# Gate stores on ScalarE and a rewritten order of the middle stage in a hybrid recurrence and pooling decoder layer

## The chip, the cores and the metric

One Trainium2 chip, one core. The metric is the time of one execution on the device in microseconds (us). Where a kernel was run several times, the median is given with the lowest and the highest. One further execution was recorded by the hardware profiler, and every duration below is from that record.

The engines go by these names: PE is the matrix engine, DVE the vector engine, ACT the scalar engine (activations and casts), POOL the general one, SP the one whose queue issues most transfers (DMAs) between the chip's memory and the core.

## What is computed

One decoder layer on 1024 tokens with 16 learned ones ahead of them, model width 1024, everything in float32:

```python
u = rmsnorm(h, mix_norm_pre)
q, f_logit, i_in, g_out, v_pool, gate_a, gate_b = split(u @ w_in)
a = hgrn2(q, f_logit, i_in, g_out, ...)      # 4 heads of 128: gated recurrence, chunked; then a norm per head, times sigmoid(g_out)
p = multiscale_pool(v_pool, pool_proj, ...)  # 4 groups of 128: trailing mean of 2, 4, 8, 16 minus identity, then a 128x128 projection
z = sigmoid(gate_a) * (a @ w_branch_hgrn) + sigmoid(gate_b) * (p @ w_branch_pool)
h = h + rmsnorm(z @ w_out, mix_norm_post)
u = rmsnorm(h, ffn_norm_pre)
y = (gelu(causal_dwconv(u @ ffn_w_gate)) * (u @ ffn_w_up)) @ ffn_w_down   # width 2816
h = h + rmsnorm(y, ffn_norm_post)            # the first 16 tokens are dropped
```

## The kernel before, in words

**Number format and tiles.** A float32 product is made of three matmuls on a high and a low part of each operand (L186 to L188, L206, L207, L210). The high part is a cast, mostly on ACT, the low part a subtraction, mostly on DVE (L832 and L833 for activations, L152/L153, L162/L163 for weights). The tokens lie along the free dimension of a tile in three chunks of about 342 to 348, each with a PSUM bank of its own (a bank holds the sums that PE writes; there are eight), and the channels lie in blocks of 128 on the partitions.

**Stages.** First the norm of the input and the projections to i. Then the gate stage, up to 326 us: f, q and the two branch gates, gate_a and gate_b, by a class `Strassen` that makes seven half-size products for eight. For each piece that is done, `put_gate` (L852 to L870) adds the partial results on DVE, applies the sigmoid on ACT (L868) to a branch gate, and has SP store the piece in the chip's memory (L870): q to `qscr`, the branch gates to `sscr`, 32 such stores. They are loaded again much later by `load_gate`. For f, `put_f` makes the decay f, the key k and kb, a product that the first level needs, and stores them. Then comes the middle stage that the change rewrites, 326 to some 650 us; after it w_out, the second norm and the feed-forward part.

**The middle stage.** PE runs in the order in which the program is written; the orders of ACT, DVE, POOL and SP are made by a scheduler that sees when things become due. The PE order is the string `ORDER` (L56 to L60). The loop at L1139 to L1178 takes a word at a time:

- `h<i>` is one more step of head i, a generator (`head_steps`, L653 to L803). It has twelve: the loads of f, q, kb and k by SP (L656 to L659), which are held until the last gate weights (for heads 0 and 1) or the last stage weights are loaded; the first level (`sb`, L719, 32x32 blocks; before it DVE multiplies q by f, L714); six levels with blocks of 2 to 64 (`sl`, L690 and L696), each of them followed by a growth of q, k and f on DVE (L673, L677, L679, L681) and a masked copy of the scores (`near`, L711); transposes (`pt`, L751); the state (`ds`, L761 to L771); the output (`po`, 34 matmuls, L781 to L794); and the norm (`ms`, L798 and L799), Ln and Exp on ACT (L800, L801), and a product on DVE (L802). L832 and L833 split o.
- `PV` is the projection of a pool group, 54 matmuls; `PVp` to `PVs` are its quarters with 18 each. `post_pv` (L809) copies the banks and makes the running sum; `sp` splits the pooled value.
- `G` is the output gate's projection of a head (quarters as above).
- `PP` is the 128x128 projection of a pool group: 9 matmuls, then ACT writes the high part (L841) and DVE the low one (L842), both to `phis`.
- `BB` and `BA` are the two branch projections, a block of 128 outputs each (`a` and `b` are halves); `post_branch` (L879) multiplies by the loaded gates `sa`. `BA` adds both.
- `sa<i>` splits head i's output for `BA`.
- `w<i>` has nothing to do with this stage: it makes ahead of time the high and low parts of weights that the feed-forward stage will need (`keep_first`, `keep_unit`, L906 to L965; DVE does L920 and L923, ACT casts at L922). `pay` (L937) stores them in memory, as `kept0` to `kept10`, through SP's queue.

In the old order the whole of PV0 (108 matmuls) stands ahead of the first head step, the four `PP` have up to two head steps between them and the `w` of the first group stand between the last `PP` and the first `BB`.

Of the kernel before, what the change touches and what calls it, by code (L numbers as in the profile page):

```python
# [11 lines left out]
AF = mybir.ActivationFunctionType  # L12
# [7 lines left out]
KD = D // P  # L20
# [32 lines left out]
ZA = 4  # L53
AHEAD = 3

ORDER = ("h0 h1 PV0 PVp1 PVq1 h0 PVr1 h1 PVs1 h0 PVp2 h1 PVq2 h0 sp0 PVr2 h1 PVs2 h0 PVp3 h1 sp1 PVq3 h0 PVr3 h1 "  # L56
# [4 lines left out]
POOLED = ()  # L61
VLOAD = 8
TRUNC = False
# [6 lines left out]
def trunk_kernel(ctx: ExitStack, tc: tile.TileContext, x, meta_tokens, mix_norm_pre,  # L70
# [3 lines left out]
    nc = tc.nc  # L74
    act, dve, pool_e, pe = nc.scalar, nc.vector, nc.gpsimd, nc.tensor
# [24 lines left out]
    def slot(n, dtype=F32, name="s"):  # L100
        return stage["fm", "p"].tile([P, n], dtype, tag="fm", name=nm(name), padded_shape=[P, LP])
# [114 lines left out]
    class Strassen:  # L216

        ORDER = ("P1", "P2", "P6", "P5", "P3", "P7", "P4")
        MOVING = dict(P1="b11", P2="b21", P3="b22", P4="t4", P5="t1", P6="t2", P7="t3")
        SECOND = ("P3", "P5", "P7")  # L220

        def __init__(self, units, run, early, quarters, base, halo, put, whole):
# [6 lines left out]
            for u in run:  # L229
                self.seq += [(u, p) for p in self.ORDER if u >= early or p not in ("P1", "P2")]  # L230
            self.got, self.at, self.kept, self.begun = [], 0, [], {}
# [385 lines left out]
    qdr = dram.tile([HEADS, P, TQ], F32, name="qscr")  # L617
# [12 lines left out]
    def put_f(m, half, g):  # L630

        n = HN if half else HF
        both = slot(2 * HP, name="fk")
        f, k = both[:, :n], both[:, HP : HP + n]
        act.activation(f, g, AF.Sigmoid)
        act.activation(k, g, AF.Sigmoid, scale=-1.0)
        dve.tensor_scalar(f, f, oml[:, m : m + 1], lb[:, m : m + 1], ALU.mult, ALU.add)
        dve.tensor_scalar(f, f, LOG_FLOOR, None, ALU.max)
        act.activation(k, k, AF.Copy, scale=oml[:, m : m + 1])
        t0 = NM + (HF if half else 0)  # L640
        for t, d in ((f, fdr), (k, kdr)):
            nc.sync.dma_start(d[m][:, t0 : t0 + n], t)
            if not half:
                nc.sync.dma_start(d[m][:, :NM], t[:, :NM])
        f2, k2 = (t[:, n - HN :].rearrange("p (b two) -> p b two", two=2) for t in (f, k))
        kb = g[:, n - HN :]
        b2 = kb.rearrange("p (b two) -> p b two", two=2)
        act.copy(b2[:, :, 0], k2[:, :, 0])
        dve.reciprocal(b2[:, :, 1], f2[:, :, 1])
        dve.tensor_tensor(b2[:, :, 1], b2[:, :, 1], k2[:, :, 1], ALU.mult)  # L650
        nc.sync.dma_start(kbdr[m][:, half * HN : half * HN + HN], kb)
# [197 lines left out]
    sd = dram.tile([2 * KD, P, TQ], F32, name="sscr")  # L849
# [3 lines left out]
    def ghalo(u):  # L853
        return NM if GUNITS[u][0] == "F" else HALO

    def put_gate(u, i, h, a, b, c=None):
        kind, j = GUNITS[u]
        m, n = 2 * j + i, ghalo(u) + HN
        at = slice(n, n + HN) if h else slice(0, n)
        g = slot(at.stop - at.start, name="sg")  # L860
        dve.tensor_tensor(g, a, b, ALU.add)
        if c is not None:
            dve.tensor_tensor(g, g, c, ALU.add)
        if kind == "F":
            put_f(m, h, g)
            return
        if kind != "Q":
            act.activation(g, g, AF.Sigmoid)  # L868
        to = dict(Q=qdr, A=sd, B=sd)[kind]
        nc.sync.dma_start(to[m + (KD if kind == "B" else 0), :, at], g)  # L870

    def load_gate(d, b, m):
        d[m] = slot(TQ, name="sa")
# [33 lines left out]
    BEGUN = [(e, p) for es in ((0, 1), (2, 3, UP0)) for p in ("P1", "P2") for e in es]  # L907
    KEPT = BEGUN + [(u, p) for u in (0, UP0) for p in Strassen.ORDER[2:]]
    kept = [[dram.tile([P, 1024], F32, name=f"kept{t}{h}") for h in "hl"] for t in range(len(KEPT) // 2)]
# [54 lines left out]

    order = ORDER.split()  # L965
    order = [(o_[:-1], int(o_[-1])) for o_ in order]
# [23 lines left out]
    def gate_steps(d):  # L990
# [10 lines left out]
        else:  # L1001
# [18 lines left out]
    ds = [slice(0, NM)] + [slice(NM + i * P, NM + (i + 1) * P) for i in range(4)]  # L1020
    gates = Strassen([(WIN, dict(F=CF, Q=CQ, A=CA, B=CB)[k] + 2 * P * j) for k, j in GUNITS], range(len(GUNITS)),
                     EARLY, gq, NM, ghalo, put_gate, lambda u, i: None)

    vb = [bank("pv") for _ in range(2)]
# [114 lines left out]
    with tc.manual_schedule(engines={E.PE}):  # L1139
        for kind, i in order:  # L1140
# [14 lines left out]
            kind, part = kind.rstrip("abpqrs"), kind[-1]  # L1155
# [548 lines left out]
    with tc.manual_schedule(engines={E.Activation, E.DVE}):  # L1704
        for s_ in range(3):
            banks = [[bank("pd") for _ in range(NT)] for _ in range(2)]
            for k in range(KH):
                at = s_ * KH + k
# [97 lines left out]
```

## Time and profile before

| what | value |
|---|---|
| time, median of 3 runs | 1319.91 us (1318.8 to 1320.88) |
| the profiled execution's own time | 1317.88 us |
| its span in the profile | 1316.2 us |
| busy PE | 1290.6 us (98%) |
| busy DVE | 961.2 us (73%) |
| busy ACT | 522.5 us (40%) |
| busy POOL | 359.9 us (27%) |
| clock granted to PE | 0.995 of full |

How to read it: the profile is of one execution, whose time is 1.68 us more than its span. PE is busy nearly all of the time, so a group of instructions on another engine counts only where PE waits for it. The share of a DMA window says how busy the sixteen transfer engines of the core were: 1.00 means full.

### The profile page before, as it was taken

To read this page: it belongs to the slowest core of one execution; us is meant where nothing else is said; L and a number is where in the kernel's file an instruction comes from. 1 tells how busy PE (TensorE), PEld (TensorE's weight loads), DVE (VectorE), ACT (ScalarE), POOL (GpSimd) and SP (SyncE) were. 2 spreads that over 40 slices of the span, in tenths; PEclk is the share of its full clock that TensorE was granted. 3 is DMA by queue.
4 is the path that set the end of the run, shared out by engine and by line. 5 is a ranking of instruction groups with operands and counts; after the bars stand their busy time and mean duration, and the time that the engine had idled before them with its cause. 6 is when DMAs were issued, how large, how long until landed. Compare 5 with 4: busy or idle time off the path is not lost.

```text
span 1316.2 us, 21988 instructions
## 1 busy us (share of the span) xinstructions
PE 1290.6 (98%) x8650; PEld 1139.7 (87%) x8650; DVE 961.2 (73%) x1293; ACT 522.5 (40%) x904; POOL 359.9 (27%) x307
## 2 busy tenths in 40 slices
PE   8999999999999899999999999999999999999998
PEld 7799899998998788978898888888888888888887
DVE  6768965454685887675588999888988985455758
ACT  5554533333134737226564222222332223444443
POOL 3015333230000000160035555554755652000000
PEclk9999999999999899999999999999999999999999
DMA  8135543334524566876677776667677699666644
GB/s 275 42 106 173 197 156 103 107 105 138 174 71 147 193 225 215 291 235 250 237 256 248 193 211 185 172 196 192 167 180 172 131 267 300 208 224 224 225 174 161
DMA packets 143802, 247.62 MB, mean 188 GB/s; under 512 B 11000, under 2 KB 75164, under 8 KB 143698
## 3 DMA queue, kind: packets, MB, share of 16 engines
q1 hardware_dynamic: 131634, 221.83, 49.6%
q0 software_dynamic: 12064, 24.38, 11.0%
q8 instruction: 68, 1.11, 0.3%
q14 instruction: 36, 0.29, 0.1%
HBM read 174.11 MB, written 95.09 MB: 205 GB/s over the span
## 4 chain that ended last, share of the span: by engine, by line
PE 91%; DVE 3%; DMA 2%; ACT 2%; issue 1%; SPq 0%; DVEq 0%; ACTq 0%
PE P L306 17%; PE P L307 17%; PE P L309 17%; PE pd L186 5%; PE pd L188 5%; PE pd L187 5%; PE pm L186 2%; PE pm L188 2%; PE pm L187 2%; PE ppv L206 1%; PE ppv L210 1%; PE pg L206 1%; PE ppv L207 1%; PE pv L187 1%; PE pv L186 1%
## 5 line engine op out<-in xcount | busy, mean ns | idle before, releaser
L307 PE MATMUL P<-v,whi 128*128 128x512 f32 (+2 forms) x408 | 140.7, 353 | 0.0
L306 PE MATMUL P<-v,whi 128*128 128x512 f32 (+2 forms) x408 | 140.7, 352 | 0.0
L309 PE MATMUL P<-v,wlo 128*128 128x512 f32 (+2 forms) x424 | 135.1, 349 | 0.0
L277 POOL TENSOR_TENSOR swa<-wraw,wraw 128x512 f32<-128x512 f32 x32 | 51.1, 1598 | 186.1 <-DMA wraw<-in_w_in_dram 79.8
L251 ACT CAST whi<-wraw 128x512 fp32r<-128x512 f32 x90 | 53.1, 618 | 102.4 <-PE P L307 75.9
L1516 DVE TENSOR_TENSOR rot<-wraw,rot 128x1024 fp32r<-128x1024 f32 x31 | 38.0, 1224 | 72.3 <-ACT rot L1515 72.3
L306 PEld LDWEIGHTS P<-v,whi 128*128 128x128 f32 x408 | 76.7, 188 | 10.4
L307 PEld LDWEIGHTS P<-v,whi 128*128 128x128 f32 x408 | 76.6, 188 | 10.2
L309 PEld LDWEIGHTS P<-v,wlo 128*128 128x128 f32 x424 | 74.0, 188 | 10.8
L187 PE MATMUL pd<-rot 128*128 128x512 f32 x274 | 82.5, 388 | 0.0
L188 PE MATMUL pd<-rot 128*128 128x512 f32 x274 | 82.5, 388 | 0.0
L186 PE MATMUL pd<-rot 128*128 128x512 f32 x274 | 81.9, 388 | 0.1
L252 DVE TENSOR_TENSOR wlo<-wraw,whi 128x512 fp32r<-128x512 f32 x86 | 76.4, 911 | 2.7 <-ACT whi L251 2.7
L251 ACT CAST whi<-swa 128x512 fp32r<-128x512 f32 x64 | 38.1, 619 | 92.6 <-PE P L307 77.8
L252 DVE TENSOR_TENSOR wlo<-swb,whi 128x512 fp32r<-128x512 f32 x64 | 66.4, 1045 | 10.4 <-ACT whi L251 10.4
L1515 ACT CAST rot<-wraw 128x1024 fp32r<-128x1024 f32 x31 | 32.7, 1054 | 90.8 <-PE pd L188 89.4
L306 PE MATMUL P<-uhi,whi 128*128 128x258 f32 (+2 forms) x240 | 68.5, 303 | 0.0
L307 PE MATMUL P<-ulo,whi 128*128 128x258 f32 (+2 forms) x240 | 68.4, 303 | 0.0
L251 ACT CAST whi<-swb 128x512 fp32r<-128x512 f32 x64 | 38.1, 618 | 71.6 <-PE P L307 67.1
L306 PE MATMUL P<-t4h,whi 128*128 128x258 f32 (+2 forms) x228 | 65.5, 304 | 0.0
L307 PE MATMUL P<-t4l,whi 128*128 128x258 f32 (+2 forms) x228 | 65.4, 304 | 0.0
L306 PE MATMUL P<-t2h,whi 128*128 128x258 f32 (+2 forms) x228 | 65.3, 304 | 0.0
(386 smaller groups left out, 3840.1 us busy)
## 6 DMA issues: line engine op xcount, KB each, us to landing
wraw<-in_w_in_dram SPq DMA_DIRECT2D x36, 512.0 KB, 4.2
yt<-ysum SPq DMA_DIRECT2D x33, 512.0 KB, 5.1
wraw<-in_ffn_w_gate_dram SPq DMA_DIRECT2D x26, 512.0 KB, 6.0
wraw<-in_ffn_w_up_dram SPq DMA_DIRECT2D x22, 512.0 KB, 6.0
wsum<-in_ffn_w_down_dram SPq DMA_DIRECT2D x22, 512.0 KB, 8.5
wraw<-in_w_out_dram SPq DMA_DIRECT2D x18, 512.0 KB, 4.4
ysum<-ys SPq DMA_DIRECT2D x11, 768.0 KB, 5.2
sa<-sscr SPq DMA_DIRECT2D x16, 513.0 KB, 5.3
```

The source lines that it names most:

```text
L186: pe.matmul(ps, ahi, bhi, start=first, stop=False)
L187: pe.matmul(ps, ahi, blo, start=False, stop=False)
L188: pe.matmul(ps, alo, bhi, start=False, stop=last)
L206: pe.matmul(ps[:, :n], whi[:, k, :], xhi, start=(k == 0), stop=False)
L251: act.copy(hi, src)
L252: (pool_e if 4 <= i < 2 * self.early else dve).tensor_tensor(lo, src, rr(hi), ALU.subtract)
L277: pool_e.tensor_tensor(s1, a21, a22, ALU.add)
L306: pe.matmul(d, whi[:, k, :], xh[:, c : c + w], start=(k == 0 and onto is None), stop=False, **go)
L307: pe.matmul(d, whi[:, k, :], xl[:, c : c + w], start=False, stop=False, **go)
L309: pe.matmul(x[:, o : o + w], wlo[:, k, :], xh[:, c : c + w], start=False, stop=(k == 3), **go)
L1515: act.copy(hi, src)
L1516: dve.tensor_tensor(lo, src, rr(hi), ALU.subtract)
```

## The change

Two things. In `put_gate` the store of a branch gate is issued from ACT's own queue, right behind the sigmoid, and no longer from SP's; the store of q stays on SP. And `ORDER` is another string: PV0 is cut in quarters and the first head steps stand after two and three of them; there is one head step between the quarters and between the pool projections; every `BB` is in halves; w0 and w1 stand after `BBb1` and `BBb2`, w4 and w5 later, w2 and w3 next to `BA2` and `BA3`.

```diff
-ORDER = ("h0 h1 PV0 PVp1 PVq1 h0 PVr1 h1 PVs1 h0 PVp2 h1 PVq2 h0 sp0 PVr2 h1 PVs2 h0 PVp3 h1 sp1 PVq3 h0 PVr3 h1 "
...
+ORDER = ("h0 h1 PVp0 PVq0 h0 PVr0 h1 PVs0 h0 PVp1 h1 PVq1 h0 PVr1 h1 PVs1 h0 sp0 PVp2 h1 PVq2 h0 sp1 PVr2 h1 PVs2 "
...
-        if kind != "Q":
-            act.activation(g, g, AF.Sigmoid)
-        to = dict(Q=qdr, A=sd, B=sd)[kind]
-        nc.sync.dma_start(to[m + (KD if kind == "B" else 0), :, at], g)
+        if kind == "Q":
+            nc.sync.dma_start(qdr[m, :, at], g)
+            return
+        act.activation(g, g, AF.Sigmoid)
+        act.dma_start(sd[m + (KD if kind == "B" else 0), :, at], g)
```

The line numbers of the changed kernel are higher by one from here on (L879 is L880 there).

On PE, inside PV0, the rows of the changed kernel (+) against the old one. `ppv` is a bank of the pool projection, `sb_3460` the first level of head 0, `q_3400` and `kb_3399` its loads.

```order
 L210 MATMUL ppv_3414<-uhi_88,wlo_3380 128x346
 L210 MATMUL ppv_3415<-uhi_88,wlo_3380 128x346
+L719 MATMUL sb_3460<-q_3400,kb_3399 32x32 x32
 L206 MATMUL ppv_3413<-uhi_88,whi_3379 128x348
 L207 MATMUL ppv_3413<-ulo_89,whi_3379 128x348
```

The first level of head 0 now stands inside the projection and was behind it before.

On SP, where the loads of head 0 (`f_3397`, `q_3400`, `kb_3399`, `k_3398`) and of head 1 (`f_3405` and on) stand, first before and then in the changed kernel. `sscr` is the memory of the branch gates, `wraw` a weight tile, `vmeta` a few values of the learned tokens.

```order
134 L149 DMA wraw_3488<-in_w_in_dram 128x8x128
135 L870 DMA sscr<-sg_3321 128x512
136 L149 DMA wraw_3666<-in_w_in_dram 128x8x128
137 L870 DMA sscr<-sg_3340 128x512
138 L656 DMA f_3397<-fscr 128x1056
139 L657 DMA q_3400<-qscr 128x1026
140 L658 DMA kb_3399<-kbscr 128x1024
141 L870 DMA sscr<-sg_3369 128x514
142 L659 DMA k_3398<-kscr 128x1056
143 L656 DMA f_3405<-fscr 128x1056
```

```order
105 L149 DMA wraw_3578<-in_w_in_dram 128x8x128
106 L149 DMA wraw_3814<-in_w_in_dram 128x8x128
107 L729 DMA vmeta_3828<-vmscr 16x128
108 L729 DMA vmeta_3895<-vmscr 16x128
109 L656 DMA f_3397<-fscr 128x1056
110 L657 DMA q_3400<-qscr 128x1026
111 L658 DMA kb_3399<-kbscr 128x1024
112 L659 DMA k_3398<-kscr 128x1056
113 L656 DMA f_3405<-fscr 128x1056
```

The gate stores are gone from among the loads, and the loads stand directly behind weight loads and two small loads of head 2 or later.

On DVE, in the stretch of the pool projections, again before and then changed. `phis` is the low part of a pool projection (L842), `k`, `q`, `f` belong to the heads, `o` and `rs` to a head's norm (L802), `al` is the split of a head's output (L833), `wlo` of L163 a branch weight and `wraw` of L923 a weight that is kept.

```order
419 L163 TENSOR_TENSOR wlo_4838<-wraw_4836,whi_4837 128x1024
420 L842 SCALAR_TENSOR_TENSOR phis_4659<-ppp_4806,par,phis_4659 128x342
421 L842 SCALAR_TENSOR_TENSOR phis_4659<-ppp_4807,par,phis_4659 128x342
422 L842 SCALAR_TENSOR_TENSOR phis_4659<-ppp_4808,par,phis_4659 128x342
423 L923 TENSOR_TENSOR wraw_4904<-wraw_4904,whi_4906 128x512 x2
424 L842 SCALAR_TENSOR_TENSOR phis_4659<-ppp_4824,par,phis_4659 128x342
425 L842 SCALAR_TENSOR_TENSOR phis_4659<-ppp_4825,par,phis_4659 128x342
426 L842 SCALAR_TENSOR_TENSOR phis_4659<-ppp_4826,par,phis_4659 128x342
427 L673 TENSOR_TENSOR k_4287<-k_4287,f_4286 128x66x8
```

```order
405 L673 TENSOR_TENSOR k_4566<-k_4566,f_4565 128x528
406 L802 TENSOR_TENSOR o_4532<-o_4532,rs_4533 128x1026
407 L681 TENSOR_TENSOR f_4565<-f_4565 128x528
408 L153 TENSOR_TENSOR wlo_4740<-wraw_4737,whi_4739 128x128
409 L673 TENSOR_TENSOR k_4354<-k_4354,f_4353 128x132x4
410 L679 TENSOR_TENSOR q_4356<-q_4356,f_4353 128x128x4
411 L711 COPY_PREDICATED near_4469<-mask_152,sl_4747 128x32x4
412 L833 TENSOR_TENSOR al_4785<-o_4433,ah_4784 128x1026
413 L681 TENSOR_TENSOR f_4353<-f_4353 128x132
414 L833 TENSOR_TENSOR al_4972<-o_4532,ah_4971 128x1026
415 L153 TENSOR_TENSOR wlo_4803<-wraw_4800,whi_4802 128x128
416 L842 SCALAR_TENSOR_TENSOR phis_4806<-ppp_4788,par,phis_4806 128x342
```

The kept weights' L923 has left the stretch; the head norm's L802 and two splits of L833 stand there ahead of the first subtraction, between steps of heads 2 and 3.

8 rows, old and new, of the table ORDER are left out of this document.

## The prediction

> **What bounds the kernel now.** I began with the page. The span and the timeline of PE, the matrix engine, come first, because the stage that the change rewrites is one in which PE is ordered by hand. I then went through PE's timeline for the whole stage, 326 to 560 us, and took out every matmul that stood behind a wait. The columns are start, duration, engine, line, operation, tile out and in, count, and in brackets the idle time just before and what ended it.
>
> ```profile
> span 1316.2 us, 21988 instructions
> ```
> ```profile
> 326.20 0.40 PE L206 MATMUL ppv<-uhi,whi 128*128 128x348 f32 x1 [0.88 <-DVE sg L861]
> ...
> 343.55 0.76 PE L719 MATMUL sb<-q,kb 128*32 128x32 f32 x64
> ...
> 425.94 0.76 PE L788 MATMUL po<-sc,vh 128*128 128x128 f32 x2 [2.00 <-DVE near L711]
> ...
> 438.14 0.42 PE L798 MATMUL ms<-rh,onesr 128*128 128x342 f32 x1 [2.55 <-DVE phis L842]
> ...
> 440.55 1.06 PE L696 MATMUL sl<-q,k 128*32 128x16 f32 x64 [1.83 <-ACT rs L800]
> ...
> 453.00 0.73 PE L696 MATMUL sl<-q,k 128*32 128x16 f32 x64 [1.51 <-DVE near L711]
> ...
> 453.89 0.42 PE L206 MATMUL pbb<-phis,whi 128*128 128x342 f32 x1 [0.16 <-ACT rs L800]
> ...
> 466.88 1.12 PE L690 MATMUL sl<-q,k 128*64 128x64 f32 x16 [1.65 <-DVE q L679]
> ...
> 492.30 0.39 PE L789 MATMUL po<-q,st 128*128 128x128 f32 x2
> 492.52 0.71 PE L751 MATMUL pt<-ident,k 128*128 128x128 f32 x5
> ...
> 497.29 1.83 PE L768 MATMUL ds<-vh,kt 128*128 128x128 f32 x14 [0.39 <-ACT kt L752]
> ...
> 503.77 0.46 PE L788 MATMUL po<-sc,vh 128*128 128x128 f32 x2 [0.57 <-DVE sa L879]
> ...
> 510.81 0.42 PE L798 MATMUL ms<-rh,onesr 128*128 128x342 f32 x1 [0.42 <-ACT rh L832]
> ...
> 512.41 0.43 PE L799 MATMUL ms<-rl,onesr 128*128 128x342 f32 x1 [1.18 <-DVE rl L833]
> ...
> 552.17 0.43 PE L206 MATMUL pba<-ah,whi 128*128 128x342 f32 x1 [1.19 <-DVE sa L879]
> ```
>
> The brackets sum to 14.33 us. PE has no other wait after its start, so all that this change can win is here, and all that it can lose is a new bracket: the matmuls are the same ones in another order. Three places hold the 14.33. The start of the stage has 0.88. A middle stretch, from the last matmul chunks of the head norms through the pool projections, has 2.00 + 2.55 + 1.83 + 1.51 + 0.16 = 8.05. The tail has 1.65 + 0.39 + 0.57 + 0.42 + 1.18 + 1.19 = 5.40.
>
> A pitch for the path follows from the same rows. Between 326.20 and 343.55 stand the 108 matmuls of PV0, so one takes 17.35 / 108 = 0.161 us. A quarter of 18 is then 2.9, about 3.05 with the change to a narrow tile and back (an estimate), and the 9 of a pool projection 1.45. A small head step of 64 narrow matmuls is taken at 0.7 (0.76 and 0.73 above). The 17 pairs of a head's output go at 492.52 − 492.30 = 0.22 to 0.23 a pair, 4.0 with its beginning.
>
> **The gate stores.** The change moves 32 stores from SP's queue to ScalarE (ACT). Here is one of the last of them with the first load of head 0 behind it and one of head 1's, then the row of the waits that shows what ACT does in that stage (total us, number of waits, longest).
>
> ```profile
> 324.60 0.32 SPq L870 DMA_DIRECT2D sscr<-sg  x1
> 324.97 0.42 SPq L656 DMA_DIRECT2D f<-fscr  x1
> ...
> 329.01 0.54 SPq L658 DMA_DIRECT2D kb<-kbscr  x1
> ```
> ```profile
> ACT whi L251 <- PE P L307: 220.8, 76, 4.4
> ```
>
> Each store stands directly behind its own sigmoid on ACT. It costs ACT 0.32 of issue and an estimated 0.1 for the sigmoid to be seen, so 32 × 0.42 = 13.4 us. What is queued behind it are the weight casts of L251 and L152, which feed PE. ACT idles 220.8 us waiting for PE ahead of those casts, so the 13.4 is covered sixteen times over, and I cost it at 0. If the cover were gone, a single store would delay a cast by 0.42. On SP the removal only frees time: nothing on PE waits on SP in the gate stage. The 0.88 at the start hangs on a DVE addition at L861 that no edit touches, so it stays, rounded to 0.9.
>
> **The first heads, begun 72 matmuls sooner.** 72 × 0.161 = 11.6 us sooner for heads 0 and 1. Their loads were in no hurry before. These are the rows at which they land (the operation that first uses each, with the wait it ended), and then three windows: stretch, its length, busy time of PE, of its weight loads, DVE, ACT and POOL with counts, PE clock, DMA share, GB/s.
>
> ```profile
> 331.51 0.69 DVE L714 TENSOR_TENSOR q<-q,f 128x512 f32<-128x512 f32 x1 [4.04 <-DMA q<-qscr]
> ...
> 335.04 0.71 DVE L673 TENSOR_TENSOR k<-k,f 128x528 f32<-128x528 f32 x1 [2.85 <-DMA k<-kscr]
> ...
> 337.70 0.69 DVE L714 TENSOR_TENSOR q<-q,f 128x512 f32<-128x512 f32 x1 [1.94 <-DMA q<-qscr]
> ...
> 341.97 0.71 DVE L673 TENSOR_TENSOR k<-k,f 128x528 f32<-128x528 f32 x1 [1.02 <-DMA k<-kscr]
> ```
> ```profile
> 322.00:324.00 2.00, 2.00 (x18) 1.92 (x17) 1.37 (x2) 0.06 (x1) 0.00 (x0) 1.00 0.69 179
> 324.00:326.00 2.00, 1.32 (x12) 1.12 (x10) 0.64 (x1) 1.40 (x2) 0.00 (x0) 1.00 1.00 321
> ...
> 334.00:336.00 2.00, 2.00 (x15) 2.00 (x14) 0.71 (x1) 0.00 (x0) 0.10 (x1) 1.00 1.02 414
> ```
>
> PE now reaches head 0's first step (sb, L719) at 326.2 + 36 × 0.161 = 332.0, and head 1's after that step and 18 matmuls, at 335.7. Head 0's q is there at 331.5 and its kb, issued next, lies between 331.5 and k's 335.0. I take 332.3, as kb stands nearer to q: a wait of 0.3. Head 1's kb lies between q's 337.7 and k's 342.0. I take the middle, 339.8. How much sooner it now comes is the doubtful number. SP is free of the six stores ahead of the loads, and their issue can go back from 324.97 to about 323.2, my estimate of when the load gate in front of them opens, since the window of 322 to 324 already has a weight load in it: 1.8 at most. But the DMA share is 1.0 from 324 on, so bytes and not issue set the landing, and only the 0.31 free share of 322 to 324 (0.6 us), with the stores' bytes gone from between the loads, gives something back. I take 1.3, so 338.5, and a wait of 338.5 − 335.7 − 0.3 (PE is already that late) = 2.5. **Sum 2.8**, with bounds of 0.2 (head 1 lands at q's time less 1.8) and 6.3 (it lands at k's 342.0).
>
> In its rules for issuing (DMA: Bandwidth & Descriptors, section "Issuing engines are not separate DMA queues") the Trainium skill says that transfers from whatever engine run on the same 16 DMA engines and interleave, and that a second issuing engine saves the sequencer's time alone. The shares of 1.00 and 1.02 above agree; by that rule alone the move buys nothing here, which is rival A below.
>
> **The middle stretch.** The two DVE weight steps w0 and w1 leave it, and the head steps and the pool projections are interleaved one to one. The prices on DVE and on ACT are these.
>
> ```profile
> 436.38 1.22 DVE L163 TENSOR_TENSOR wlo<-wraw,whi 128x1024 fp32r<-128x1024 f32 x1
> 437.52 1.53 DVE L842 SCALAR_TENSOR_TENSOR phis<-ppp,par,phis 128x342 fp32r<-128x342 f32 x3
> 438.96 1.28 DVE L923 TENSOR_TENSOR wraw<-wraw,whi 128x512 fp32r<-128x512 f32 x2
> ...
> 441.67 0.71 DVE L673 TENSOR_TENSOR k<-k,f 128x528 f32<-128x528 f32 x1
> ...
> 443.77 1.23 DVE L802 TENSOR_TENSOR o<-o,rs 128x1026 f32<-128x1026 f32 x1 [0.58 <-ACT rs L801]
> ...
> 449.99 1.29 DVE L920 TENSOR_TENSOR wlo<-wraw,wraw 128x512 f32<-128x512 f32 x2 [3.59 <-DMA wraw<-in_ffn_w_gate_dram]
> ...
> 452.64 1.26 DVE L833 TENSOR_TENSOR al<-o,ah 128x1026 fp32r<-128x1026 f32 x1
> ```
> ```profile
> 439.95 1.42 ACT L800 ACTIVATE rs<-ms,eps_t 128x342 f32<-128x342 f32 x3
> 441.39 1.28 ACT L801 ACT_TABLE_LOAD   x1
> 442.68 1.06 ACT L801 ACTIVATE rs<-rs 128x1026 f32<-128x1026 f32 x1
> ```
>
> Back to back, an operation takes its duration less some 0.08 (436.38 to 437.52 is 1.14 for a row of 1.22). Two waits come out of this.
>
> First, head 3's first step now follows head 0's norm closely on DVE. From the end of the norm's matmuls run Ln 1.35, table 1.28, Exp 1.0, L802 1.14, then the decay step L681 0.55 and L714 0.6, together 5.95. PE meanwhile has a level step 0.7, a gate quarter 3.05 and the other norm's 6 matmuls 1.0, together 4.7. The wait is 1.25, and I take **1.4** for one crossing between the engines.
>
> Second, from that step to the first branch product BBa0, DVE must do what BBa0's accumulator waits for: the subtractions of PP2 on L842. In its new queue that is 3 × 3 of L842 (3 × 1.45 = 4.35), L802 (1.15), two L833 (2.4), two L163 (2.3), four L673 and three L679 (7 × 0.62 = 4.3), four masks, three decay steps and two small splits of 0.2 to 0.6 (3.4): 17.9, and one crossing of 0.7 with 0.9 of idle while masks wait for PE's levels, 19.5. PE has in the same time the head step 0.7, the last gate quarter 3.05, five small steps at 0.67 and four pool projections at 1.45: 12.9. The waits between sum to **6.6**, whichever instructions show them.
>
> **Sum 8.0**, against 8.05 before. So 3.86 us of weight work (L923 twice, L920 once) is gone from DVE there, but the same stretch of PE is shorter by head steps that are now done earlier, and L802 and both L833 of heads 0 and 1 are now inside it. Lower bound: DVE gets L802 and the two L833 done in its idle time, −3.5, 4.5. Upper bound: ACT reloads its table twice more on the path, 2 × 1.28, 10.6.
>
> On the table load the Trainium skill (ScalarE: Activation LUTs, section "What ACT_TABLE_LOAD costs") has 1283 ns and a drain of 1380 ns more for every switch. The trace agrees with the first alone: the load of 441.39 is followed by Exp at 442.68, 1.29 later, and nothing stands between. With the drain the norm's chain would be 1.4 longer and the forecast 1321.0; the rows decide.
>
> **The tail.** Here the later weight steps and the kept stores matter: name, queue, count, KB each, median us from issue to landing.
>
> ```profile
> kept7h<-whi SPq DMA_DIRECT2D x2, 256.0 KB, 2.0
> kept7l<-wlo SPq DMA_DIRECT2D x2, 256.0 KB, 4.4
> ...
> kept2l<-wraw SPq DMA_DIRECT2D x2, 256.0 KB, 8.1
> ```
>
> The step w4 stands between two steps of head 2 and a branch half, and its L920 waits on DVE for a load, as in the row above (3.59 idle there, no PE wait behind it). I take 0.7 for PE at BBa4, bounds 0 and 3.6. The norm of head 3 then waits for the norm of head 2 and for a weight tile to be stored before DVE may overwrite it. The chain: Ln, table, Exp 3.65, L802 1.15, three sums of L879 1.3 (as L842 × 3), a weight part 0.6, the store 4.4, two more parts 1.3, L794 1.2 and L833 1.1 (both priced as L833): 14.7. PE has two branch halves at 3.0, the output pairs at 4.0 and a third and partial products of another 3.0: 13.0. Wait **1.7**. **Sum 2.4** against 5.40, bounds 0.5 (a store of 2.0 removes the 1.7) and 6.1 (a store of 8.1 adds 3.7).
>
> **The total.** 0.9 + 2.8 + 8.0 + 2.4 = 14.1 us against 14.3: −0.2 to −0.3, so 1317.6 for a run that took 1317.88 when it was profiled. That run lies 1.68 above its span and 2.03 below the median of the three runs, 1319.91. On the scale of the median the forecast is **1319.6 us**, no measurable change (about 0.2%, 2.6 us, is what can be told from none). The three groups' bounds are −2.6/+3.5, −3.5/+2.6 and −1.9/+3.7; they are unlikely to fall together, their squares add to −4.8/+5.7, and the case's own four fifths are some 1316.5 to 1323. With the rivals the range becomes **1315.0 to 1324.0**.
>
> **The rivals.**
> *A, slower: the loads do not come sooner.* The DMA engines are full from 324, so head 1's kb lands as before, at up to 342.0, and the early start runs into it: 6.3 − 2.8 = +3.5, 1323.1. It decides once kb lands after 341. Against it speaks the free share before 324. Chance 0.18.
> *B, slower: the kept store is slow.* At 8.1 instead of 4.4, head 3's norm waits 3.7 longer, 1323.3. It needs landing times over 7; two of the three rows above lie far below. Chance 0.12.
> *C, faster: the weight work was what the stretch waited for.* DVE has 3.86 less to do between 436 and 452, and if all of it comes off the 8.05 there with nothing late next, the time is 1315.7. For it: the waits at 438.14 and 453.00 both name DVE. Against it: ACT's Ln ended 1.83 of it, and the interleave puts L802 and L833 in the place. Chance 0.28.
> That the change does not do what it says is no case: the instructions stand in the order described. Forecast: 0.42. So faster by over 0.2% has 0.28, within 0.2% 0.42, slower 0.30.
>
> **What would show it.** PE's waits at sb of head 1 (2.5, ended by kb's load), at sb of head 3 (1.4), at the pool projections and BBa0 (6.6 together, L842) and at the norm of head 3 (1.7, L833) prove or break each step; so does SP's first L656 at about 323. No wait of PE should name a weight cast delayed by a store. The forecast is wrong if the sum of PE's brackets differs from 14 by over 2.6, and wrong in kind if time appears outside this stage, where PE has none to lose.

## The result and the profile after

The changed kernel takes 1314.48 us (median of 5 runs, 1312.12 to 1315.53) against 1320.25 (5 runs, 1318.80 to 1320.88): a ratio of 0.9955, with a 95% interval of 0.994 to 0.997, 4 to 8 us faster. The forecast was no measurable change, 1319.6, with a range from 1315.0. The profiled execution took 1315.28, so it is one of the slower ones, and the profiled one of before, at 1317.88, was faster than all five of those. The two traces are therefore only 2.6 apart.

PE's timeline of the changed kernel, every matmul that stood behind a wait from 326 us on:

```profile
span 1313.6 us, 21972 instructions
```
```profile
327.30 0.40 PE L206 MATMUL ppv<-uhi,whi 128*128 128x348 f32 x1 [0.88 <-ACT whi L152]
...
335.32 0.75 PE L719 MATMUL sb<-q,kb 128*32 128x32 f32 x64 [2.07 <-DMA kb<-kbscr]
...
342.12 0.75 PE L719 MATMUL sb<-q,kb 128*32 128x32 f32 x64 [1.45 <-DMA kb<-kbscr]
...
431.41 0.90 PE L719 MATMUL sb<-q,kb 128*32 128x32 f32 x64 [2.03 <-ACT rs L800]
...
442.89 0.42 PE L206 MATMUL ppp<-plh,whi 128*128 128x342 f32 x1 [0.99 <-DVE phis L842]
...
444.55 0.39 PE L206 MATMUL ppp<-plh,whi 128*128 128x342 f32 x1 [1.08 <-DVE near L711]
...
447.51 0.65 PE L206 MATMUL ppp<-plh,whi 128*128 128x342 f32 x1 [0.39 <-DVE phis L842]
...
451.15 1.05 PE L696 MATMUL sl<-q,k 128*32 128x16 f32 x64 [0.21 <-DVE near L711]
...
565.99 0.47 PE L186 MATMUL pm<-whi,zc 128*128 128x512 f32 x1 [0.69 <-DVE sa L880]
```

The places of the forecast are all there (heads 0 and 1, head 3, the pool projections), but the tail, from the first branch product at 452 us, has only the 0.69 at its very end.

Brackets alone do not tell the loss. The windows of both kernels show the granted PE clock (third figure from the end of each row). First before, then after:

```profile
425.00:442.00 17.00, 11.67 (x186) 10.94 (x187) 16.31 (x26) 12.95 (x23) 0.95 (x1) 0.82 0.64 210
442.00:452.00 10.00, 9.49 (x110) 8.95 (x109) 5.83 (x11) 4.43 (x7) 0.00 (x0) 0.80 0.66 223
452.00:569.00 117.00, 110.44 (x1028) 106.27 (x1029) 89.72 (x155) 52.35 (x89) 6.14 (x4) 1.00 0.69 235
```
```profile
326.00:340.00 14.00, 11.05 (x119) 10.58 (x118) 6.09 (x8) 1.60 (x2) 2.12 (x6) 0.88 1.00 352
...
425.00:442.00 17.00, 14.87 (x365) 13.72 (x352) 12.62 (x19) 14.66 (x23) 0.18 (x3) 0.90 0.47 155
442.00:452.00 10.00, 7.44 (x150) 5.89 (x150) 10.00 (x21) 7.10 (x13) 0.00 (x0) 0.67 0.87 277
452.00:569.00 117.00, 116.31 (x963) 112.78 (x956) 93.97 (x162) 49.79 (x89) 8.41 (x5) 1.00 0.73 252
```

Behind some of the gaps PE runs at half clock for about 3.4 us or twice that. The shares give what that takes at most (some of the slow time falls into PE's idle time): before 17 × 0.18 + 10 × 0.20 = 5.1 us, after 14 × 0.12 + 17 × 0.10 + 10 × 0.33 = 6.7. The half clock is thus not what the change saved: the changed kernel lost more that way than the old one. With it the stage reads so, from the opening matmul to the first of w_out:

| place | brackets before | half clock before | brackets after | half clock after | forecast after |
|---|---|---|---|---|---|
| heads 0 and 1 begin | 0 | 0 | 3.52 | 1.7 | 2.8 |
| up to the first branch product | 6.38 | 3.1 | 4.70 | 5.0 | 8.0 |
| from there on | 7.07 | 2.0 | 0.69 | 0 | 2.4 |

The forecast's borders differ in one point: it counted the old waits of 1.51 and 0.16, which stand behind the first branch product, in its middle stretch.

The stage itself went from 242.5 us (326.20 to 568.7) to 238.7 (327.30 to 566.0), 3.8 less. What the span holds outside the stage is 1073.7 us before and 1074.9 after, and 1073.6 to 1075.1 in all fourteen traces of this case. Most of the 1.1 us by which the stage opens later has a reason outside the change, one DVE instruction in the gate stage, long before the first gate store (176.46 us on SP before, 177.13 on ACT after). POOL's addition L277 starts beside it. First before, then after:

```profile
112.10 0.56 DVE L637 TENSOR_SCALAR fk<-fk,oml,lb 128x528 f32<-128x528 f32 x1 [0.71 <-ACT fk L635]
...
112.33 1.49 POOL L277 TENSOR_TENSOR swa<-wraw,wraw 128x512 f32<-128x512 f32 x1 [3.59 <-DMA wraw<-in_w_in_dram]
```
```profile
112.02 1.68 DVE L637 TENSOR_SCALAR fk<-fk,oml,lb 128x528 f32<-128x528 f32 x1 [0.71 <-ACT fk L635]
...
112.11 1.30 POOL L277 TENSOR_TENSOR swa<-wraw,wraw 128x512 f32<-128x512 f32 x1 [3.45 <-DMA wraw<-in_w_in_dram]
```

### The profile page after: what moved, and what is told of

Read it like the earlier page. It is cut to its first block, busy times and chain, and to the rows that moved or that the text cites. A ratio compares the mean times of both kernels' runs of the same rounds, so it can differ in the third digit from the quotient of the medians.

```text
span 1313.6 us, 21972 instructions
## 1 busy us (share of the span) xinstructions
PE 1291.5 (98%) x8650; PEld 1140.3 (87%) x8650; DVE 963.7 (73%) x1293; ACT 524.8 (40%) x905; POOL 355.1 (27%) x307
## 4 chain that ended last, share of the span: by engine, by line
PE 92%; DMA 2%; DVE 2%; ACT 2%; issue 1%; SPq 0%; DVEq 0%; ACTq 0%
PE P L306 16%; PE P L307 16%; PE P L309 16%; PE pd L186 5%; PE pd L188 5%; PE pd L187 5%; PE pm L186 2%; PE pm L188 2%; PE pm L187 2%; PE pbb L206 1%; PE pbb L210 1%; PE ppv L206 1%; PE pbb L207 1%; PE pv L187 1%; PE pba L206 1%; PE pba L210 1%
## 5 line engine op out<-in xcount | busy, mean ns | idle before, releaser
L277 POOL TENSOR_TENSOR swa<-wraw,wraw 128x512 f32<-128x512 f32 x32 | 48.2, 1506 | 191.0 <-DMA wraw<-in_w_in_dram 79.4
```

Of the source, the lines that this page charges most:

```text
L277: pool_e.tensor_tensor(s1, a21, a22, ALU.add)
```

## The experiments

Each was profiled and run in five rounds beside the kernel before on the same chip, and the ratios are to that kernel (0.0010 is 1.3 us). Two experiments on different chips are best compared by these ratios. Line numbers can be off by one or by a few where an edit shifts them.

**Stores alone, and the order alone.** The old `ORDER` with the new `put_gate`, and the new `ORDER` with the old `put_gate`.

> The old order, with only the gate stores moved to ScalarE. First theory (the new order alone saves the time; ScalarE has idle time ahead of its casts): within 1 us of the kernel before, PE's waits of the middle stage the same 13 to 14 us and the same three periods at half clock. Rival (the stores out of SP's queue are what helps, since the head loads issue sooner): 2 to 6 us faster than before, with loads of heads 0 and 1 landing over 1 us sooner.

> The new order, with the gate stores left on SP. First theory: as fast as the changed kernel, at most 1.3 us slower, which is what I had put down for the loads of head 1 coming sooner. By the rule that all transfers share the same engines, no difference at all and the same landing of kb. Rival (the stores carry the gain): 3 us or more slower than the changed kernel.

Stores alone: 1319.19, 0.9998 (0.9988 to 1.0007), the first theory. In its trace the loads of heads 0 and 1 are issued 2.2 us sooner than before (324.97 there), and head 1's q lands 0.7 sooner (337.70 there):

```profile
322.75 0.68 SPq L655 DMA_DIRECT2D f<-fscr  x1
...
337.02 0.69 DVE L713 TENSOR_TENSOR q<-q,f 128x512 f32<-128x512 f32 x1 [1.80 <-DMA q<-qscr]
```

Order alone: 1316.23, 0.9974 (0.9963 to 0.9984). Its loads are issued 1.7 us later than the changed kernel's 324.59, and the first levels start at 6.96 and 14.34 from the stage's opening matmul at 327.49 (the changed kernel's at 8.02 and 14.82):

```profile
326.27 0.43 SPq L656 DMA_DIRECT2D f<-fscr  x1
...
334.45 0.75 PE L719 MATMUL sb<-q,kb 128*32 128x32 f32 x64 [1.00 <-DMA kb<-kbscr]
...
341.83 0.75 PE L719 MATMUL sb<-q,kb 128*32 128x32 f32 x64 [3.58 <-DMA kb<-kbscr]
```

Single traces differ more than that. The runs below with the weights put back, with the old tail and with the bunched steps have the words of the changed kernel for heads 0 and 1, and there head 1's first level starts 13.34, 12.94 and 13.00 from the opening, in the changed kernel 14.82. The 14.34 lies among them, so no effect of the issue on kb is shown. The Trainium skill (DMA: Bandwidth & Descriptors, section "Issuing engines are not separate DMA queues") states that issuing from a second engine saves only the time of the issue. The time of the stores alone agrees (0.9998), though head 1's q did land a little sooner there. The order carries the gain; the medians of this run and of the changed kernel are 1.75 apart, between the two theories, but their intervals overlap, so no gain of the stores is shown.

**The first heads later.** The words of PV0 and PV1:

```diff
-h0 h1 PVp0 PVq0 h0 PVr0 h1 PVs0 h0 PVp1 h1 PVq1 h0 PVr1 h1 PVs1 h0 sp0
+h0 h1 PVp0 PVq0 PVr0 PVs0 h0 PVp1 h1 PVq1 h0 PVr1 h1 h0 PVs1 h1 h0 sp0
```

> The changed kernel with the first steps of heads 0 and 1 two quarters (36 matmuls) later, caught up by the end of the second pool projection; everything behind is as in the changed kernel. Theory that the early start is a plain loss (waits of 2.07 and 1.45 for kb, and about 1.7 of half clock after the first of them): 3.5 to 5.2 us faster than the changed kernel. Rival (the catch-up meets DVE and the waits return a few steps later): within 1 us of it.

1310.79, 0.9926 (0.9912 to 0.9940): about 3.8 us faster than the changed kernel, the first theory. Both waits are gone, and the steps that were caught up bring only a gap of 0.50 for which the profile names no cause. Head 3's first level comes 99.07 us after the stage's opening at 326.52, against 104.11. At the end of the stage 2.4 of these 5.0 are left (236.3 us against 238.7): head 3's wait is as it was, half clock runs on to 450.1, some 3.4 us into the branch products, and the last wait is 1.53 against 0.69:

```profile
425.59 0.78 PE L719 MATMUL sb<-q,kb 128*32 128x32 f32 x64 [2.03 <-ACT rs L800]
...
562.79 0.47 PE L186 MATMUL pm<-whi,zc 128*128 128x512 f32 x1 [1.53 <-DVE sa L880]
```

The early start is thus a loss, and the rest of the new order more than pays for it.

**What sets that loss.** Two runs: dummy matmuls in the waits, and head 0's k behind head 1's kb.

```diff
         ps = bank("sb")
+        if h < 2:
+            jb = bank("pj")
+            for _ in range((10, 12)[h]):
+                pe.matmul(jb[:, :P], onesm, ident, start=True, stop=True)
```
```diff
             nc.sync.dma_start(kb[:, M0:], kbdr[h])
-            nc.sync.dma_start(k, kdr[h])
+            late.append((k, kdr[h]))
+            while late and h:
+                nc.sync.dma_start(*late.pop(0))
```

> The changed kernel with matmuls that nobody reads put on PE directly ahead of the first level of head 0 (10) and of head 1 (12), at 0.18 us each (28 of them took 5.16 at the start of the span), in the places where PE stood still for 2.07 and 1.45. Theory that PE's clock is halved for about 3.4 us after such a gap and that this costs 1.7 on top of the bracket: the brackets at both first levels nearly vanish, no period at half clock follows there, and the time falls by about 1.7, less what the filling overshoots the waits by (up to 0.5). Rival (the half clock costs nothing there, or has another cause): the time is as before or up to 0.5 longer, or the period at half clock stays.

> The changed kernel with the load of head 0's k (128x1056, 541 KB) put behind head 1's kb. Theory that bytes in the queues, not issue, set when kb lands: at the 400 GB/s that the full windows show, 541 KB are 1.35 us, so head 1's first level starts 1.3 us sooner and the time falls by up to that, unless k itself becomes late for the level after. Rival (issue or a landing time of its own sets it): no change of that start.

The filled kernel takes 1314.58, 0.9958 (0.9943 to 0.9972): no gain. No half clock is left there, and yet head 1's first level comes 15.03 after the opening at 326.50, no sooner than 14.82. The filling took 2.39 and 2.84 us where 1.8 and 2.2 were meant, so this level stands right behind it and the trace does not show when kb landed:

```profile
332.30 2.39 PE L718 MATMUL pj<-ident,onesm 128*128 128x128 f32 x20
335.11 0.75 PE L723 MATMUL sb<-q,kb 128*32 128x32 f32 x64 [0.41 <-DMA kb<-kbscr]
...
338.76 2.84 PE L718 MATMUL pj<-ident,onesm 128*128 128x128 f32 x24
...
341.53 0.76 PE L723 MATMUL sb<-q,kb 128*32 128x32 f32 x64
```

At this place my theory that the half clock costs 1.7 of its own falls: in the changed kernel PE still waits 1.45 for head 1's kb behind the slow time, so at full clock it would have waited longer instead. With the weights put back there is no half clock between the two levels, and the second wait is 2.79. What counts is the landing. By the forecast's pitch that level would stand 9.5 after the opening; it stands at 12.9 to 14.8 in the four traces with these words, so the early start loses 3.4 to 5.3.

With k later the time is 1311.67, 0.9934 (0.9921 to 0.9946). Head 0's level still waits 2.74, head 1's no longer, and it comes at 13.97 (341.11 less the opening at 327.14), 0.85 sooner:

```profile
335.84 0.75 PE L723 MATMUL sb<-q,kb 128*32 128x32 f32 x64 [2.74 <-DMA kb<-kbscr]
```

That is less than the spread of 12.94 to 14.82 among the traces with unchanged loads, so an effect of the bytes in the queues is not shown. The medians are 2.8 apart, their intervals overlap a little, and where that gain comes from, if it is one, stays open.

**The half clock by itself.** In the kernel with the later first heads, a gap where PE is otherwise never late:

```diff
+            if (kind, part, i) == ("PV", "p", 2):
+                jb, ja = bank("pj"), bank("pj")
+                ga, gb = small([P, 8], "ga", "ga", 1), small([P, 8], "gb", "gb", 1)
+                pe.matmul(jb[:, :P], ident, ident, start=True, stop=True)
+                act.copy(ga, jb[:, :8])
+                for _ in range(3):
+                    dve.tensor_scalar(gb, ga, 1.0, None, ALU.mult)
+                    act.copy(ga, gb)
+                pe.matmul(ja[:8, :P], ga, ident, start=True, stop=True)
```

> The kernel with the later first heads, with a gap made on PE at the start of the third pool projection: a small matmul, seven copies of 8 columns passed between ScalarE and DVE, and a matmul that needs the last. There PE has no wait. An added bracket of 1.5 to 2.5 us. Theory that such a gap brings PE to half clock for about 3.4 us and that this costs where PE has no other wait to absorb it: slower than the kernel with the later first heads by the bracket plus 1.7, with windows at 0.5 behind it. Rival: slower by the bracket alone.

1322.62, 1.0023 (1.0012 to 1.0033), 0.0097 or 12.8 us above the kernel without the gap. The gap came out far longer than meant, as the copies queued behind DVE's other work. The matmul behind it, and a window of the time after:

```profile
365.57 0.59 PE L1177 MATMUL pj<-ident,ga 128*8 128x128 f32 x2 [10.61 <-ACT ga L1176]
```
```profile
369.00:371.00 2.00, 2.00 (x9) 2.00 (x8) 0.00 (x0) 0.00 (x0) 0.00 (x0) 0.50 0.00 0
```

Nine matmuls in 2 us, and 14 in the window of 373 to 375. Finer windows put the half clock from 357.5, within the gap, to 371.2: 13.7 us, or four times 3.4. The quarter behind the gap took from 366.09 to 371.43, 5.3 us where 3.05 is usual, and from the stage's opening to the first gate matmul it is 13.2 us longer (399.22 − 326.07 = 73.15, against 386.47 − 326.52 = 59.95). That is the bracket of 10.6, 2.3 of slow quarter and the added matmuls. So where nothing else is waited for, the slow time does cost. How long a gap must be for it is not settled by this run: a gap of 2.03 to 2.05 at head 3's first level was followed by half clock in the changed kernel, and in three others (order alone, k later, old tail) not.

Where another engine is late the slow time costs nothing, as the filled kernel shows a second time. In its pool projections PE keeps full clock in the very window in which the changed kernel has 0.67:

```profile
442.00:452.00 10.00, 6.21 (x154) 4.82 (x155) 10.00 (x20) 6.83 (x13) 0.00 (x0) 1.00 0.88 276
```

Its first branch product stands 124.74 us from the opening all the same, the changed kernel's 124.83, and the stage takes 238.9 against 238.7. DVE is busy for 10.00 of these 10 us in both, so a faster PE only waits longer.

**The weight steps.** w0 and w1 back ahead of the first branch product in the changed kernel; and in the kernel before, w0, w1 and the first w4 moved back.

```diff
-PP3 h2 BBa0 h3 ... BBb1 h2 w0 BBa2 h3 BBb2 h2 w1 BBa3
+PP3 h2 w0 w1 BBa0 h3 ... BBb1 h2 BBa2 h3 BBb2 h2 BBa3
```
```diff
-h2 w0 w1 BBa0 w4 h3 ... BBb1 h2 sa1 BBa2 ... BBb2 h3 BBa3 h2 h3 BBb3
+h2 BBa0 h3 ... BBb1 h2 w0 sa1 BBa2 ... BBb2 h3 w1 BBa3 h2 h3 w4 BBb3
```

> The changed kernel with w0 and w1 put back between the last pool projection and the first branch product. Theory that the weight work on DVE was what the old stretch waited for: 2.6 us slower than the changed kernel (two pairs of L924 at 1.28), up to 4.3 if a further period at half clock follows. Theory that the even spread of head steps saves the time: 0 to 0.7 us slower, as the two pairs stand behind the last subtraction that the first branch product needs.

> The kernel before, its gate stores on SP, with only w0, w1 and the first w4 moved back behind the first branch products. Theory that the weight work on DVE was what the stretch waited for: 2 to 3.9 us faster than before, since 3.86 us of DVE work leave the 8.05 us of waits. Rival (two of its four waits stand ahead of that work, and the head steps set them): 0 to 1.5 us faster, with the 2.00 and the 2.55 still there.

Put back in the changed kernel: 1317.46, 0.9980 (0.9970 to 0.9990), some 3 us slower than the changed kernel (its interval touches that kernel's), with a new wait behind the first branch products:

```profile
462.49 0.74 PE L696 MATMUL sl<-q,k 128*32 128x16 f32 x64 [1.29 <-DVE sa L880]
```

Moved back in the kernel before: 1318.39, 0.9992 (0.9982 to 1.0002), no difference that can be told. The waits only move:

```profile
425.67 0.46 PE L787 MATMUL po<-sc,vh 128*128 128x128 f32 x2 [2.03 <-DVE near L710]
...
439.39 0.42 PE L797 MATMUL ms<-rh,onesr 128*128 128x342 f32 x1 [3.92 <-ACT rs L799]
...
500.20 0.38 PE L780 MATMUL po<-scm,vmeta 16*128 16x2 f32 x2 [2.54 <-DVE st L770]
```

The 1.51 at 453.00 is gone, for it stood behind the first w4. The last wait shown is new and stands behind weight work again: DVE idles for a store of kept weights to land before the additions of the state that PE needs.

```profile
496.01 1.29 DVE L919 TENSOR_TENSOR wlo<-wraw,wraw 128x512 f32<-128x512 f32 x2 [3.93 <-DMA kept7l<-wlo]
```

Weight work counts where DVE is the one that is late. Moving these three words alone did not free the old order of it; whether another place for them would is not tested.

**The tail.** First the old words from the first branch product on, then the new ones with only the steps of heads 2 and 3 in the old places. Three steps of these heads fewer are left there than in the old order, so the first four halves, which held steps in the old order, have none in these two runs.

```diff
-BBa0 h3 BBb0 h2 BBa1 h3 BBb1 h2 w0 BBa2 h3 BBb2 h2 w1 BBa3 h3 h2 w4 BBb3 ...
+w0 w1 BBa0 w4 BBb0 w4 BBa1 BBb1 h2 BBa2 h3 h2 BBb2 h3 BBa3 h2 h3 BBb3 ...
```
```diff
-BBa0 h3 BBb0 h2 BBa1 h3 BBb1 h2 w0 BBa2 h3 BBb2 h2 w1 BBa3 h3 h2 w4 BBb3 ...
+BBa0 BBb0 BBa1 BBb1 h2 w0 BBa2 h3 h2 BBb2 h3 w1 BBa3 h2 h3 w4 BBb3 ...
```

> The changed kernel up to the last pool projection, and from the first branch product on the words in the old order (weight steps w0, w1, w4 at once, the steps of heads 2 and 3 late and then two at a time between halves). Theory that the even spread of head steps over the branch products is where the time comes from (the waits behind 441 us fell from 7.07 and some half clock to 0.69): 5 us or more slower than the changed kernel, with waits at transposes, states, outputs and norms of heads 2 and 3 back. Rival (the heads being further along at the first branch product does it): at most 1 us slower.

> The changed kernel with the weight steps where the change put them, and only the steps of heads 2 and 3 among the branch products in the old places (none in the first four halves, then two at a time). Theory that the spread of the head steps is what the change gains among the branch products: 3 us or more slower than the changed kernel, with waits of PE at levels, states and outputs of heads 2 and 3. Rival (the weight steps put early are what cost the 6 us of the run with the old tail): within 1.3 us of the changed kernel.

The old tail: 1320.57, 1.0004 (0.9993 to 1.0014). The whole gain is gone. PE waits again for heads 2 and 3:

```profile
467.98 1.91 PE L690 MATMUL sl<-q,k 128*64 128x64 f32 x16 [2.94 <-DVE q L679]
...
500.40 1.83 PE L768 MATMUL ds<-vh,kt 128*128 128x128 f32 x14 [0.92 <-ACT kt L752]
...
507.25 0.49 PE L788 MATMUL po<-sc,vh 128*128 128x128 f32 x2 [0.94 <-DVE sa L880]
...
519.58 0.42 PE L206 MATMUL pbb<-phis,whi 128*128 128x342 f32 x1 [1.25 <-ACT rs L800]
```

The bunched steps with the new weight steps: 1319.24, 0.9986 (0.9972 to 1.0000). By the ratios 0.0031 of the loss of 0.0049, about two thirds, is there without any weight step being moved:

```profile
478.54 0.70 PE L690 MATMUL sl<-q,k 128*32 128x32 f32 x32 [1.13 <-DVE q L679]
...
500.62 1.83 PE L768 MATMUL ds<-vh,kt 128*128 128x128 f32 x14 [0.98 <-ACT kt L752]
...
519.94 0.42 PE L206 MATMUL pbb<-phis,whi 128*128 128x342 f32 x1 [2.04 <-ACT rs L800]
```

So most of the gain hangs on the even spread of the head steps over the branch products: the heads being further along at the first branch product, which these two runs share with the changed kernel, does not bring it alone. Whether the loss comes from the four halves without steps or from the pairs behind them was not separated.

**The middle stretch relieved.** On the kernel with the later first heads: `sa0` and `sa1` moved from the pool projections to the halves `BBa4` and `BBa5`; and then also head 3 begun sooner.

```diff
-Gs3 h2 sa0 PP0 h3 PP1 h2 PP2 h3 sa1 PP3 ... BBb3 h3 BBa4 h2 BBb4 h3 w4 BBa5
+Gs3 h2 PP0 h3 PP1 h2 PP2 h3 PP3 ... BBb3 h3 sa0 BBa4 h2 BBb4 h3 sa1 w4 BBa5
```
```diff
-h0 h2 Gp3 h1 h3 Gq3 h0 h2 Gr3 h1 h3 Gs3
+h0 h3 h2 Gp3 h1 Gq3 h3 h0 h2 Gr3 h1 Gs3
```

> The kernel with the later first heads, and with the splits of the outputs of heads 0 and 1 (two L833 of 1.23 on DVE) moved out of the pool projections to the fourth and fifth branch products. Theory that DVE's queue bounds that stretch: the waits there, 0.99 + 1.08 + 0.54 + 0.51, shrink by up to 2.4, and if a period at half clock goes too, 4.1 in all. Rival (PE at half clock or ACT bounds it): under 0.7.

> As the run before, and head 3 begun two quarters sooner, so that its q times f (L714) stands ahead of head 0's L802 on DVE. Theory: the wait of 2.03 at head 3's first level goes, and with it about 1.7 of half clock: 2.0 to 3.7 faster than the run before. Rival (its loads are not there in time, or the work comes back as waits in the pool projections): within 1 us of it.

1310.86, 0.9929 (0.9909 to 0.9949), with runs from 1306.85 to 1314.99, and 1310.57, 0.9929 (0.9913 to 0.9944): neither is faster than the later first heads alone. (By the words, head 3's first level of the last run stands one quarter and three head steps sooner.) In the last, head 3's wait of 2.03 is gone, and PE meets this instead:

```profile
433.87 0.39 PE L206 MATMUL ppp<-plh,whi 128*128 128x342 f32 x1 [0.85 <-DVE near L711]
...
436.91 0.42 PE L206 MATMUL ppp<-plh,whi 128*128 128x342 f32 x1 [1.35 <-DVE phis L842]
...
444.65 0.65 PE L206 MATMUL pbb<-phis,whi 128*128 128x342 f32 x1 [2.69 <-ACT scm L737]
```

The rival was right: what is taken away there comes back a step later. DVE is busy without a break there too (9.00 of the 9 us from 436 to 445 in the first run, 7.00 of the 7 from 434 to 441 in the last), which speaks for its queue as the bound; no run tests that against the handing to and fro between DVE and ACT.

Several versions beat both kernels. The simplest is the one with the later first heads, at 1310.79.

## Why the prediction was wrong, point by point

- **"All that this change can win is here", the 14.33 us of brackets.** This step failed. I counted the old stage by its brackets and the new one by how late PE would be against its pitch, and a slow clock makes PE late too. Counted alike, the old stage was up to 18.5 us late behind its opening wait (13.45 of brackets and 5.1 at half clock) where I had 13.45, and the changed one 15.6 (8.91 and 6.7) where I had 13.2. So there was something to win where the forecast saw nothing. By the sign that I had named it failed as well: the brackets of after sum to 9.8 with the opening's, not to 14. The clock stood in the rows of the windows from which I had taken the DMA share. This does not make the half clock a price of its own in the old stage. Behind its second slow time (to 446) DVE stood idle for 3.59 at the first w4, and the copy behind that ended PE's 1.51 at 453.00. I had written that no PE wait stands behind this idle time; one does.

```profile
452.42 0.43 DVE L711 COPY_PREDICATED near<-mask,sl 128x128 f32<-128x128 uint8 x1
```

- **The tail, forecast at 2.4 against 5.40.** Mis-sized: 0.69, as the two new waits that I forecast did not come. Measured from the first branch product on, with the clock, it is 0.69 against 9.1, a gain of 8.4 where I had put down 3.0; the difference in the base is the half clock (2.0) and the 1.67 that I had counted in the middle stretch. For the norm of head 3 I had a store of 4.4 in the chain. In the trace it is issued at 507.02, lands in 2.1, the part behind it starts at 509.17 (the row names a copy on ACT, but that had ended at 508.65), and the last subtraction ends at 512.80, 0.3 before PE gets there at 513.09:

```profile
507.02 0.32 SPq L938 DMA_DIRECT2D kept7l<-wlo  x1
```
```profile
509.17 1.29 DVE L924 TENSOR_TENSOR wlo<-wraw,whi 128x512 fp32r<-128x512 f32 x2 [2.18 <-ACT o L791]
...
511.58 1.22 DVE L833 TENSOR_TENSOR rl<-rs,rh 128x1026 fp32r<-128x1026 f32 x1
```

  That is the lower end that the bounds named (a store of 2.0). That most of the gain goes without the spread is what the old tail and the bunched steps show.
- **The first heads, forecast at 2.8.** Right in kind, too small: 5.3 in the trace of after, 3.4 to 5.3 in the four with these words. I took 1.3 off the landing for sooner issue; the mean of the four, 13.5 from the opening, is the 13.6 that I had without it. Rival A, a landing as before, came true in part and was outweighed. The later first heads give back 3.8. (The 108 matmuls that stood ahead of the first step in the old order are the 72 of PV0 and half of PV1; the 72 by which the step moved are right.)
- **The middle stretch, forecast at 8.0.** The sum held: from head 3's first level at 431.41 to the first branch product at 452.13 it is 20.7 us, forecast 19.5. Of the 6.6 forecast behind head 3 only 2.67 shows as brackets; the rest appears as a slow clock, in the place of waits for DVE. But the old stretch, too, lost 3.1 at half clock beside its brackets. Head 3's wait was 2.03, forecast 1.4, and by the forecast's chain: the row names Ln (L800), but the product L714 behind head 0's L802 ends last, at 431.31, 0.10 before the level starts.

```profile
430.63 0.68 DVE L714 TENSOR_TENSOR q<-q,f 128x512 f32<-128x512 f32 x1
```

- **Stores at nothing.** Right, 0.9998 by themselves.
- **Rival C, the weight work.** It had the right sign for the whole, but its mechanism is not shown: in the old order moving that work changes nothing that can be told, and in the new one putting two of its words back costs some 3 us of the gain. Rival B did not come: the store took 2.1.
- **The scale.** I placed the forecast on the profiled run plus 2.03. That run was faster than the five that the result compares; the traces show 3.8 for the stage, the medians 5.8. The 2 us between them are within what runs of one kernel differ here, and are not traced to a cause.

## What to carry to other kernels

Price a wait by when the waiting engine is through with the work behind it, at the clock it then has, and not by the bracket; and check the old kernel's base in the same way before saying how much there is to win. A step that is slowed in front of a later wait costs nothing as long as that wait does not hang on the step: ask for the arrival that decides (here the landing of head 1's kb, and DVE's queue in the pool projections). Where a dependent chain runs beside a stream of matmuls, spread its steps singly over the stream, and begin it only when its data is there.

## What the runs showed of the hardware that I had not expected

- Behind gaps of 2 us and more PE often ran at a granted clock of 0.50, for 3.4 us or a multiple, 9 matmuls in 2 us instead of 14. It did not follow every such gap. Two shorter gaps in a row were followed by it too: 0.99 and 1.08 in the changed kernel by 6.8 us from 445.5 on, while the same two in the filled kernel (0.98 and 1.08) were not. The Trainium skill (TensorE: Matmul & The Clock Gate, section "What's actually happening") has a window of some 3.4 us that runs freely, half rate after an idle one and full rate after a busy one. The traces agree on 0.50 and on the 3.4. They differ on the gap: the same page (section "HAM oscillation — how this bites in real kernels") warns of gaps over about 3.4, and here 2.00 (before, at 425.94) and 2.03 were enough. That a window running freely makes it a matter of chance which gap is caught would fit the gaps of 2.04 and 2.05 that were not followed, but no run here shows it.
- DVE's L637 (128x528) took 0.56 us in nine traces and 1.48 to 1.68 in five, with the same DVE instructions in front of it. It goes with POOL: in the five, POOL's addition L277 starts from 0.11 before to 0.09 after L637, in the nine 0.11 to 0.41 after it. No run changes POOL's start by itself.
- The same loads landed at different times from one execution to the next: head 1's first level, which waits for them, stood 12.94 to 14.82 us from the opening in four traces with the same words for heads 0 and 1. So a difference of less than 2 us there between two single traces shows no effect.
